# Loading and splitting the first weight and input tiles in a stated order, with a second-half weight buffer of its own

## The chip, the cores and the metric

One core of a Trainium2 chip runs the whole kernel in one launch. The metric is device time in microseconds of an execution; a kernel's time is the median of its runs. The engines are named as in the profile: PE (TensorE, matmuls), PEld (its weight loads), DVE (VectorE), ACT (ScalarE), POOL (GpSimd) and SP (SyncE, which here only issues DMAs). ACT issues DMAs too.

## The reference, cut to what matters

A layer over 1024 tokens of width 1024. The part around the change is the first RMSNorm and the input projection; after it come window attention, neighbourhood attention, an output projection and a gated MLP, which stay as they are.

```python
def rmsnorm(x, g):
    xf = x.astype(jnp.float32)
    y = xf * lax.rsqrt(jnp.mean(xf * xf, axis=-1, keepdims=True) + EPS)
    return (y * g.astype(jnp.float32)).astype(x.dtype)
...
    hn = rmsnorm(h, norm_mix[l])
    proj = jnp.einsum('bsd,de->bse', hn, w_in[l])
```

## The kernel before, in words

**Products in three matmuls.** A float32 operand is split in a high part (a copy on ACT to the type float32r) and a low part (on DVE: the value less its high part). A product of a 128x128 weight block and a 128x512 block of x is then three matmuls (`block`, L143 to L146): high by high, high by low, low by high.

**The head.** x comes transposed, as eight tiles `xt` of 128 x 1024 (k = 0 to 7, each with two halves h of 512 tokens). The first two output tiles of the projection, `first`, are computed side by side, in PSUM banks named `pj` (tile 0) and `o` (tile 1): for each k, for each h, for each of the two tiles, one `block`. That is 96 matmuls. The gain of the norm is multiplied into x as it is split (`split_x` for k = 0 and 1 in halves, `split_scaled` for the rest, giving `xgh` and `xgl`); the inverse root of the mean square is multiplied in when the banks are read out. So the squares of all x tiles are summed beside it (`squares`, L166: a square `sq` on ACT, an add on DVE), reduced on PE (`ss`, L181), rooted on ACT and inverted on DVE (`v`, L184 and L185), spread over the partitions on PE (`sw`, L192) and copied to `rstd1` (L626), which every read-out needs. Between them PE runs the third output tile (banks `s`): its first half before `ss`, 3 of its blocks between `ss` and `sw`, the rest after.

**Weights.** The first halves of the weights of the two tiles (k = 0 to 3) are in `head`, loaded by ACT's queue in four DMAs (L103) and split by `first_w`. The second halves (k = 4 to 7) go through `load_w` (L140): a raw buffer of tag `raw`, which has two slots, then a high and a low buffer of tags `whi` and `wlo`, which have three slots each (L135). A slot is taken again when its last reader is done.

**Order.** PE runs in program order. The other engines' and the queues' order is set by a scheduler, from priorities and its own estimates; each engine then runs its list in order and stops at an instruction whose data or buffer isn't ready. A DMA also waits for the landing of the one eight before it. The warm-up matmuls (L114, WARM of them) run on PE ahead of the data.

**What stands next to it.** `nsink` (L592) is made on DVE from the sinks; POOL copies it into probability tiles (L348). POOL also builds the bias tiles `xb` (L426 and L427, `bias_tiles`) from `rr`, a load of 244.5 KB by SP (L418) into one single buffer. The next weights (projections 3 and 4) are loaded by SP at L130 and split at L136 and L137; on ACT the first split for projection 4 stands just ahead of the root `v`.

Of the kernel before, what the change touches and what calls it, by code (L numbers as in the profile page):

```python
# [13 lines left out]
F32 = mybir.dt.float32  # L14
F32R = mybir.dt.float32r
AF = mybir.ActivationFunctionType
ALU = mybir.AluOpType
PSUM = bass.MemoryType.PSUM

D, S, HD = 1024, 1024, 64  # L20
KT = D // 128
# [6 lines left out]
EPS = 1e-6  # L28
# [6 lines left out]
SPARE = (3, 6)  # L35
AHEAD = 2
EVA = (1, 3, 5, 8)
WARM = 8

REST = 11  # L40

# [6 lines left out]
C_NMIX, C_NFFN, C_NFIN, C_NA, C_NB, C_CW, C_CB, C_SINK = 0, 8, 16, 24, 28, 32, 98, 120  # L48
C_END = 128
# [4 lines left out]
def hybrid_layer(tc, xT, w_in, w_out, w_gate, w_up, w_down, small, sink, rpb, consts, rope, out):  # L54
    nc = tc.nc
    with ExitStack() as ctx:
        pool = lambda name, bufs, **kw: ctx.enter_context(tc.tile_pool(name=name, bufs=bufs, **kw))
        cpool = pool("const", 1)
# [4 lines left out]
        wpool = inner("weights", 3)  # L63
# [6 lines left out]
        def big(name, tag, dt=F32):  # L70
            return lpool.tile([128, S], dt, name=name, tag=tag, bufs=slots[tag])

        def tmp(name, dt=F32, n=S):
            return tpool.tile([128, n], dt, name=name, tag="t", padded_shape=[128, S + 2])

        def bank(name, tag):
            return psum.tile([128, HALF], F32, name=name, tag=tag)

        f32 = lambda ap: ap.bitcast(F32)
        tsl = lambda h: slice(h * HALF, (h + 1) * HALF)  # L80
        col = lambda c: par[:, c:c + 1]

        par = cpool.tile([128, C_END], F32, name="par")
        nc.scalar.dma_start(par[:, 0:C_SINK], small)
        ones = cpool.tile([128, 128], F32, name="ones")
        nc.gpsimd.memset(ones, 1.0 / D)
        eps = cpool.tile([128, 1], F32, name="eps")
        nc.gpsimd.memset(eps, EPS)
        cst = cpool.tile([128, K_END], F32, name="cst")
        ident = cst[:, K_ID:K_ID + 128]  # L90


        def load_x(k, parts=1):
            xt = big("xt", "op")
            n = S // parts
            for i in range(parts):
                nc.sync.dma_start(xt[:, i * n:(i + 1) * n], xT[k, :, i * n:(i + 1) * n])
            return xt

        head = [[wpool.tile([128, 4, 128], dt, name="w0", tag=tag, bufs=n) for dt, tag, n in ((F32, "raw", 2), (F32R, "whi", 3), (F32R, "wlo", 3))] for _ in range(2)]  # L100
        for ks in (slice(0, 1), slice(1, 4)):
            for m, (raw, _, _) in enumerate(head):
                nc.scalar.dma_start(raw[:, ks], w_in[m, :, ks, :])  # L103
        xts = [load_x(0, 2), load_x(1, 2)]


        ctx.enter_context(tc.manual_schedule(engines={mybir.EngineType.PE}))


        warm = cpool.tile([128, 1], F32, name="warm")  # L110
        nc.scalar.activation(warm, eps, AF.Square)
        warm_ps = psum.tile([128, HALF], F32, name="warm_ps", tag="pt")
        for _ in range(WARM):
            nc.tensor.matmul(warm_ps[:, 0:128], ones, ones, start=True, stop=True)  # L114
# [12 lines left out]
        def fetch_w(src):  # L127

            raw = wpool.tile([128, 4, 128], F32, name="raw", tag="raw", bufs=2)
            nc.sync.dma_start(raw, src)  # L130
            return raw

        def halve_w(raw):

            hi, lo = (wpool.tile([128, 4, 128], F32R, name=n, tag=n) for n in ("whi", "wlo"))  # L135
            mark["weights"] = nc.scalar.activation(hi, raw, AF.Copy)  # L136
            mark["weights low"] = nc.vector.tensor_tensor(lo, raw, f32(hi[:, :, :]), op=ALU.subtract)  # L137
            return [(hi[:, j, :], lo[:, j, :]) for j in range(4)]

        def load_w(src):  # L140
            return halve_w(fetch_w(src))

        def block(ps, w, x, h, first, last):  # L143
            nc.tensor.matmul(ps, w[0], x[0][:, tsl(h)], start=first, stop=False)  # L144
            nc.tensor.matmul(ps, w[0], x[1][:, tsl(h)], start=False, stop=False)  # L145
            nc.tensor.matmul(ps, w[1], x[0][:, tsl(h)], start=False, stop=last)  # L146
# [6 lines left out]

        def split_scaled(src, scale, name, tag):
            hi, lo = big(name + "h", tag, F32R), big(name + "l", tag, F32R)
            nc.scalar.activation(hi, src, AF.Copy, scale=scale)
            nc.vector.scalar_tensor_tensor(lo, src, scale, f32(hi[:, :]), op0=ALU.mult, op1=ALU.subtract)
            return hi, lo

        def split(src, name, tag):  # L160
            hi, lo = big(name + "h", tag, F32R), big(name + "l", tag, F32R)
            nc.scalar.activation(hi, src, AF.Copy)
            nc.vector.tensor_tensor(lo, src, f32(hi[:, :]), op=ALU.subtract)
            return hi, lo

        def squares(tiles, engine):  # L166
            acc = None
            for t in tiles:
                s2 = tmp("sq")
                nc.scalar.activation(s2, t, AF.Square)  # L170
                if acc is not None:
                    engine.tensor_tensor(s2, s2, acc, op=ALU.add)
                acc = s2
            return acc
# [114 lines left out]
        mix = [None] * 8  # L289
# [269 lines left out]
        xg, first = [None] * KT, [Project(0), Project(1)]  # L559

        def split_x(k, h):

            g = col(C_NMIX + k)
            hi, lo = (t[:, tsl(h)] for t in xg[k])
            nc.scalar.activation(hi, xts[k][:, tsl(h)], AF.Copy, scale=g)
            nc.vector.scalar_tensor_tensor(lo, xts[k][:, tsl(h)], g, f32(hi), op0=ALU.mult, op1=ALU.subtract)

        def first_w(ks):
            for raw, hi, lo in head:
                nc.scalar.activation(hi[:, ks], raw[:, ks], AF.Copy)  # L570
                nc.vector.tensor_tensor(lo[:, ks], raw[:, ks], f32(hi[:, ks]), op=ALU.subtract)

        for k in range(2):
            xg[k] = big("xgh", "xg", F32R), big("xgl", "xg", F32R)
        split_x(0, 0)
        first_w(slice(0, 1))
        split_x(0, 1)
        first_w(slice(1, 4))
        for h in range(2):
            split_x(1, h)  # L580
        for p, (_, hi, lo) in zip(first, head):
            p.w = [(hi[:, j, :], lo[:, j, :]) for j in range(4)]
        for k in range(2, 4):
            xts.append(load_x(k))
        for p in first:
            p.w += load_w(w_in[p.m, :, 4:8, :])
        for k in range(4, KT):
            xts.append(load_x(k))
        nc.sync.dma_start(cst, consts)
        nc.sync.dma_start(par[:, C_SINK:C_END], sink.partition_broadcast(128))  # L590
        nsink = cpool.tile([128, 8], F32, name="nsink")
        nc.vector.tensor_scalar(nsink, par[:, C_SINK:C_END], -1.0, None, op0=ALU.mult)  # L592
        quarters = lambda t: t[:, :].rearrange("p (a s w) -> p a s w", a=4, s=2)
        turns = quarters(big("turns", "mix"))
        rc, rs = turns[:, 0], turns[:, 1]
        nc.sync.dma_start(turns[:, 0:2], rope)
        t = quarters(big("f", "mix"))
        folded += [(t[:, 0], t[:, 1]), (t[:, 2], t[:, 3]), (turns[:, 2], turns[:, 3])]

        banks = [[bank("pj", "pj") for _ in range(2)], [bank("o", "o") for _ in range(2)]]  # L600
        acc = None
        for k in range(KT):
            if k > 1:
                xg[k] = split_scaled(xts[k], col(C_NMIX + k), "xg", "xg")
            for h in range(2):
                for p, ps in zip(first, banks):
                    block(ps[h], p.w[k], xg[k], h, k == 0, k == KT - 1)
        acc = squares(xts, nc.vector)
        jobs = [Project(m) for m in range(2, 18)] + [OutA(d) for d in range(KT)]
        third = jobs[0]  # L610
        raw, hi, lo = big("raw3", "mix"), big("whi3", "mix", F32R), big("wlo3", "mix", F32R)
# [114 lines left out]
        for g in range(2):  # L726
            for b in range(NB):
                q, t = unit_window(g, b)
# [49 lines left out]
        for u in range(len(flat)):  # L778
            q, t, need, kind = flat[u]
# [49 lines left out]
        for h in range(2):  # L829
            wide = widen(vb2[h], "pt")  # L830
            for i in range(4):
                x = mix[4 + i][:, tsl(h)]
                hi, lo = (t[:, tsl(h)] for t in mg[4 + i])
# [303 lines left out]
        raws, dws, xs, xraw, kept, sum_tiles = {}, {}, {}, {}, {}, {}  # L1137
# [116 lines left out]
        sq, todo, vs = {}, [], {}  # L1254
# [57 lines left out]
        for i, (p, j, c) in enumerate(order):  # L1312
            prepare(i + 6, i + 4)
            f, n = PARTS[c]
# [30 lines left out]
        parts = {}  # L1345
# [15 lines left out]
        first = quarters[1].start  # L1361
# [96 lines left out]
```

## Time and profile before

| | |
|---|---|
| runs | 1103.87, 1103.57, 1101.68 us; median 1103.57 |
| profiled execution | 1103.74 us, of which 1101.9 us from the first to the last instruction (span) |
| granted TensorE clock, mean | 0.996 |
| busy share of the span | PE 98%, PEld 82%, DVE 78%, ACT 50%, POOL 10% |
| DMA | 144.95 MB moved |

A row of the timeline has the start and the duration in us, the engine (a q behind it: its queue of DMA issues), the line in the kernel, the operation, what it writes and reads, its shape and count, and in brackets how long the engine stood idle before it and what ended that. A row of windows has the stretch, its length, the busy time and the number of instructions for PE, PEld, DVE, ACT and POOL, then the granted clock, the DMA engines' busy share and GB/s.

### The profile page before, as it was taken

Reading aid. Unit: us, or ns where it says so; the run is one execution under the profiler, and the core shown is the slowest. Engines: PE = TensorE matmul, PEld = TensorE weight load, DVE = VectorE, ACT = ScalarE, POOL = GpSimd, SP = SyncE. Lnnn points to the kernel's source line nnn. Section 1 sums busy time; section 2 is a strip of 40 time slices with the busy share of each in tenths; the row PEclk is TensorE's granted clock in tenths of the full one; section 3 lists DMA queues with packets and bytes.
Section 4 is the critical chain, followed back from the end, with each engine's and each line's share of the span. In section 5 each row is a group of like instructions: output and inputs, shape, how many; then the busy total and the mean of one; then the engine's idle time right before and its main releaser. Section 6 shows DMA issues by size and latency. Waiting matters only on the chain.

```text
span 1101.9 us, 15051 instructions
## 1 busy us (share of the span) xinstructions
PE 1079.2 (98%) x5190; PEld 901.0 (82%) x5190; DVE 858.5 (78%) x1565; ACT 552.9 (50%) x1042; POOL 109.2 (10%) x188
## 2 busy tenths in 40 slices
PE   8999999999999999999999999999999999999996
PEld 6888788888888888887788888888888778888886
DVE  7688787667688689899988877887787857886843
ACT  7457676556676544545434343433434643533631
POOL 2223333222232100000000000000000000000001
PEclk9999999999999999999999999999999999999998
DMA  7222122222225136214342232322233888774824
GB/s 271 72 72 68 48 58 68 77 76 77 77 67 159 68 127 240 96 39 162 124 161 89 104 124 77 132 98 106 96 112 109 277 288 289 258 227 165 270 79 154
DMA packets 68365, 144.95 MB, mean 132 GB/s; under 512 B 8128, under 2 KB 18880, under 8 KB 68288
## 3 DMA queue, kind: packets, MB, share of 16 engines
q1 hardware_dynamic: 57632, 118.16, 33.6%
q10 hardware_dynamic: 10656, 25.82, 6.2%
q8 instruction: 41, 0.67, 0.2%
q14 instruction: 36, 0.29, 0.1%
HBM read 103.58 MB, written 28.57 MB: 120 GB/s over the span
## 4 chain that ended last, share of the span: by engine, by line
PE 86%; DVE 7%; DMA 3%; ACT 2%; issue 2%; POOL 0%; SPq 0%; DVEq 0%; ACTq 0%; POOLq 0%
PE pj L144 7%; PE pj L145 7%; PE pj L146 7%; PE dn L866 6%; PE dn L867 6%; PE dn L868 6%; PE z L868 5%; PE z L866 5%; PE z L867 5%; PE x L866 3%; PE s L327 3%; PE x L867 3%; PE x L868 3%; PE y L868 3%; PE y L867 3%; PE y L866 3%
## 5 line engine op out<-in xcount | busy, mean ns | idle before, releaser
L866 PE MATMUL dn<-xd,whi 128*128 128x512 f32 (+1 forms) x330 | 124.9, 378 | 2.3 <-ACT c L1294 2.3
L868 PE MATMUL dn<-xd,wlo 128*128 128x512 f32 (+1 forms) x330 | 124.4, 377 | 0.0
L867 PE MATMUL dn<-xd,whi 128*128 128x512 f32 (+1 forms) x330 | 124.2, 377 | 0.0
L855 ACT ACTIVATE whi<-ws 128x512 fp32r<-128x512 f32 (+1 forms) x100 | 60.2, 624 | 122.3 <-DVE ws L972 80.4
L866 PE MATMUL z<-hg,whi 128*128 128x512 f32 x264 | 103.0, 390 | 1.0 <-DVE gs L1022 1.0
L144 PE MATMUL pj<-xgh,whi 128*128 128x512 f32 x248 | 104.0, 419 | 0.0
L868 PE MATMUL z<-hg,wlo 128*128 128x512 f32 x264 | 103.1, 390 | 0.6 <-DVE wlo L856 0.6
L867 PE MATMUL z<-hg,whi 128*128 128x512 f32 x264 | 102.7, 389 | 0.0
L353 ACT ACTIVATE p<-p,nm 128x385 f32<-128x385 f32 (+3 forms) x128 | 75.3, 588 | 51.7 <-DVE nm L349 50.6
L146 PE MATMUL pj<-xgh,wlo 128*128 128x512 f32 x248 | 97.6, 393 | 0.0
L145 PE MATMUL pj<-xgl,whi 128*128 128x512 f32 x248 | 97.2, 392 | 0.0
L357 POOL TENSOR_SCALAR p<-p,sm 128x384 f32<-128x384 f32 (+1 forms) x128 | 74.1, 591 | 215.9 <-DVE sm L355 201.5
L856 DVE TENSOR_TENSOR wlo<-raw,whi 128x512 fp32r<-128x512 f32 (+1 forms) x102 | 66.6, 673 | 22.7 <-ACT whi L855 22.4
L363 DVE TENSOR_TENSOR pl<-pt,ph 128x384 fp32r<-128x384 f32 (+2 forms) x108 | 63.0, 588 | 24.5 <-ACT ph L362 23.2
L855 ACT ACTIVATE whi<-raw 128x512 fp32r<-128x512 f32 (+1 forms) x102 | 60.5, 613 | 42.7 <-DMA raw<-in_w_down_dram 19.3
L856 DVE TENSOR_TENSOR wlo<-ws,whi 128x512 fp32r<-128x512 f32 (+1 forms) x100 | 66.8, 683 | 18.7 <-ACT whi L855 18.7
L1285 POOL TENSOR_TENSOR h<-h,wide 128x256 f32<-128x256 f32 (+1 forms) x6 | 5.4, 920 | 718.7 <-ACT wide L1281 718.7
L1177 ACT ACTIVATE xd<-xd 128x512 fp32r<-128x512 f32 x77 | 47.1, 627 | 55.0 <-DMA xd<-x 53.5
L866 PEld LDWEIGHTS dn<-xd,whi 128*128 128x128 f32 x330 | 62.5, 189 | 14.0 <-ACT c L1294 2.8
L868 PEld LDWEIGHTS dn<-xd,wlo 128*128 128x128 f32 x330 | 62.4, 189 | 11.5
L867 PEld LDWEIGHTS dn<-xd,whi 128*128 128x128 f32 x330 | 62.5, 190 | 11.1
L362 ACT ACTIVATE ph<-pt 128x384 fp32r<-128x384 f32 (+2 forms) x108 | 55.2, 515 | 32.0 <-PE pt L462 25.0
(211 smaller groups left out, 2686.0 us busy)
## 6 DMA issues: line engine op xcount, KB each, us to landing
xd<-x SPq DMA_DIRECT2D x77, 256.0 KB, 5.1
raw<-in_w_down_dram SPq DMA_DIRECT2D x72, 256.0 KB, 3.4
raw<-in_w_gate_dram SPq DMA_DIRECT2D x22, 512.0 KB, 3.6
raw<-in_w_up_dram SPq DMA_DIRECT2D x22, 512.0 KB, 3.8
x<-c ACTq DMA_DIRECT2D x22, 512.0 KB, 2.6
raw<-in_w_in_dram SPq DMA_DIRECT2D x32, 256.0 KB, 3.0
raw<-in_w_down_dram SPq DMA_DIRECT2D x36, 192.0 KB, 3.9
x<-t ACTq DMA_DIRECT2D x11, 512.0 KB, 2.6
```

The costliest lines, as they stand in the source:

```text
L144: nc.tensor.matmul(ps, w[0], x[0][:, tsl(h)], start=first, stop=False)
L145: nc.tensor.matmul(ps, w[0], x[1][:, tsl(h)], start=False, stop=False)
L146: nc.tensor.matmul(ps, w[1], x[0][:, tsl(h)], start=False, stop=last)
L353: nc.scalar.activation(p[:, j, 0:e], p[:, j, 0:e], AF.Exp, bias=nm, scale=-1.0, accum_out=sm[:, j:j + 1])
L357: nc.gpsimd.tensor_scalar(p[:, i, 0:m], p[:, i, 0:m], sm[:, i:i + 1], 1.0, op0=ALU.mult, op1=ALU.mult)
L362: nc.scalar.activation(ph[:, 0:n], ps[:, 0:n], AF.Copy)
L363: nc.vector.tensor_tensor(pl[:, 0:n], ps[:, 0:n], f32(ph[:, 0:n]), op=ALU.subtract)
L855: nc.scalar.activation(hi, src, AF.Copy)
L856: nc.vector.tensor_tensor(lo, src, f32(hi[:, :, :]), op=ALU.subtract)
L866: nc.tensor.matmul(ps, w[0], x[0], start=first and i == 0, stop=False, skip_group_check=True)
L867: nc.tensor.matmul(ps, w[0], x[1], start=False, stop=False, skip_group_check=True)
L868: nc.tensor.matmul(ps, w[1], x[0], start=False, stop=last and i == len(ws) - 1, skip_group_check=True)
```

## The change

All x tiles and weights of the head are queued in one stated order, and `tc.keep_in_program_order` (`pin`) keeps the marked instructions of a queue or an engine in the order in which the program states them.

- The four first-half weight DMAs move from ACT's queue to SP's, behind the first half of x tile 0; the second half of x tile 0 moves to ACT's queue.
- The second halves of both tiles' weights are loaded into a buffer of their own, `second` (one of the eight slots of tag `mix`), each behind its x tile (2 and 3). They are still split by `halve_w`, into `whi` and `wlo`.
- x is split for k = 2 to 7 ahead of the matmul loop; with each of k = 4 to 7 go two squares and their adds (`add_square`), in place of `squares` after the loop.
- `nsink` and the loads of the constants are pinned too, in the place where the program has them.
- WARM goes from 8 to 9.

```diff
-WARM = 8
+WARM = 9
...
+        pin = tc.keep_in_program_order
         par = cpool.tile([128, C_END], F32, name="par")
+        xts = [big("xt", "op") for _ in range(KT)]
+
+        def load_x(k, part=slice(0, S), queue=nc.sync):
+            pin(queue.dma_start(xts[k][:, part], xT[k, :, part]))
+
+        second = big("raws", "mix")[:, :].rearrange("p (m k c) -> p m k c", m=2, c=128)
+        load_x(0, tsl(0))
         nc.scalar.dma_start(par[:, 0:C_SINK], small)
+        load_x(0, tsl(1), nc.scalar)
+        for ks in (slice(0, 1), slice(1, 4)):
+            for m, (raw, _, _) in enumerate(head):
+                pin(nc.sync.dma_start(raw[:, ks], w_in[m, :, ks, :]))
+        load_x(1, tsl(0))
+        load_x(1, tsl(1))
+        for k in (2, 3):
+            load_x(k)
+            pin(nc.sync.dma_start(second[:, k - 2], w_in[k - 2, :, 4:8, :]))
+        for k in range(4, KT):
+            load_x(k)
...
+        def add_square(t, acc):
+            s2 = tmp("sq")
+            pin(nc.scalar.activation(s2, t, AF.Square))
+            if acc is not None:
+                pin(nc.vector.tensor_tensor(s2, s2, acc, op=ALU.add))
+            return s2
...
         for k in range(2, 4):
-            xts.append(load_x(k))
-        for p in first:
-            p.w += load_w(w_in[p.m, :, 4:8, :])
+            xg[k] = split_scaled(xts[k], col(C_NMIX + k), "xg", "xg")
+            first[k - 2].w += halve_w(second[:, k - 2])
+        added = None
         for k in range(4, KT):
-            xts.append(load_x(k))
-        nc.sync.dma_start(cst, consts)
-        nc.sync.dma_start(par[:, C_SINK:C_END], sink.partition_broadcast(128))
+            xg[k] = split_scaled(xts[k], col(C_NMIX + k), "xg", "xg")
+            for i in range(2 * k - 8, 2 * k - 6):
+                added = add_square(xts[i], added)
+        pin(nc.sync.dma_start(cst, consts))
+        pin(nc.sync.dma_start(par[:, C_SINK:C_END], sink.partition_broadcast(128)))
         nsink = cpool.tile([128, 8], F32, name="nsink")
-        nc.vector.tensor_scalar(nsink, par[:, C_SINK:C_END], -1.0, None, op0=ALU.mult)
+        pin(nc.vector.tensor_scalar(nsink, par[:, C_SINK:C_END], -1.0, None, op0=ALU.mult))
...
         for k in range(KT):
-            if k > 1:
-                xg[k] = split_scaled(xts[k], col(C_NMIX + k), "xg", "xg")
             for h in range(2):
                 for p, ps in zip(first, banks):
                     block(ps[h], p.w[k], xg[k], h, k == 0, k == KT - 1)
-        acc = squares(xts, nc.vector)
+        acc = added
```

In the changed kernel the line numbers are 7 higher from the helpers on, and 14 higher behind `add_square`; the split of weights is at L143 and L144, that of x at L163 and L164, the squares at L175 and their adds at L177, the bias loads at L432.

More of the change, by code (lines that the diff above doesn't have):

```diff
@@ L81, in hybrid_layer @@
         col = lambda c: par[:, c:c + 1]
+        pin = tc.keep_in_program_order
         par = cpool.tile([128, C_END], F32, name="par")
-        nc.scalar.dma_start(par[:, 0:C_SINK], small)
+        xts = [big("xt", "op") for _ in range(KT)]
+        def load_x(k, part=slice(0, S), queue=nc.sync):
+            pin(queue.dma_start(xts[k][:, part], xT[k, :, part]))
+        head = [[wpool.tile([128, 4, 128], dt, name="w0", tag=tag, bufs=n) for dt, tag, n in ((F32, "raw", 2), (F32R, "whi", 3), (F32R, "wlo", 3))] for _ in range(2)]
+        second = big("raws", "mix")[:, :].rearrange("p (m k c) -> p m k c", m=2, c=128)
+        load_x(0, tsl(0))
+        nc.scalar.dma_start(par[:, 0:C_SINK], small)
+        load_x(0, tsl(1), nc.scalar)
[9 more added lines that the diff above has]
+            load_x(k)
+        cst = cpool.tile([128, K_END], F32, name="cst")
+        ident = cst[:, K_ID:K_ID + 128]
+        ctx.enter_context(tc.manual_schedule(engines={mybir.EngineType.PE}))
         ones = cpool.tile([128, 128], F32, name="ones")
@@ L88, in hybrid_layer @@
         nc.gpsimd.memset(eps, EPS)
[L89 to L107, printed above, removed]
         warm = cpool.tile([128, 1], F32, name="warm")
-        nc.scalar.activation(warm, eps, AF.Square)
+        pin(nc.scalar.activation(warm, eps, AF.Square))
         warm_ps = psum.tile([128, HALF], F32, name="warm_ps", tag="pt")
@@ L155, in split_scaled @@
             hi, lo = big(name + "h", tag, F32R), big(name + "l", tag, F32R)
-            nc.scalar.activation(hi, src, AF.Copy, scale=scale)
-            nc.vector.scalar_tensor_tensor(lo, src, scale, f32(hi[:, :]), op0=ALU.mult, op1=ALU.subtract)
+            pin(nc.scalar.activation(hi, src, AF.Copy, scale=scale))
+            pin(nc.vector.scalar_tensor_tensor(lo, src, scale, f32(hi[:, :]), op0=ALU.mult, op1=ALU.subtract))
             return hi, lo
@@ L564, in split_x @@
             hi, lo = (t[:, tsl(h)] for t in xg[k])
-            nc.scalar.activation(hi, xts[k][:, tsl(h)], AF.Copy, scale=g)
-            nc.vector.scalar_tensor_tensor(lo, xts[k][:, tsl(h)], g, f32(hi), op0=ALU.mult, op1=ALU.subtract)
+            pin(nc.scalar.activation(hi, xts[k][:, tsl(h)], AF.Copy, scale=g))
+            pin(nc.vector.scalar_tensor_tensor(lo, xts[k][:, tsl(h)], g, f32(hi), op0=ALU.mult, op1=ALU.subtract))
         def first_w(ks):
             for raw, hi, lo in head:
-                nc.scalar.activation(hi[:, ks], raw[:, ks], AF.Copy)
-                nc.vector.tensor_tensor(lo[:, ks], raw[:, ks], f32(hi[:, ks]), op=ALU.subtract)
+                pin(nc.scalar.activation(hi[:, ks], raw[:, ks], AF.Copy))
+                pin(nc.vector.tensor_tensor(lo[:, ks], raw[:, ks], f32(hi[:, ks]), op=ALU.subtract))
         for k in range(2):
@@ L595, in hybrid_layer @@
         rc, rs = turns[:, 0], turns[:, 1]
-        nc.sync.dma_start(turns[:, 0:2], rope)
+        pin(nc.sync.dma_start(turns[:, 0:2], rope))
         t = quarters(big("f", "mix"))
@@ L600, in hybrid_layer @@
         banks = [[bank("pj", "pj") for _ in range(2)], [bank("o", "o") for _ in range(2)]]
-        acc = None
         for k in range(KT):
-            if k > 1:
-                xg[k] = split_scaled(xts[k], col(C_NMIX + k), "xg", "xg")
             for h in range(2):
```

## The prediction

> **What bounds the kernel now.** I read the page first, then busy time by stretch for the first 61 us, which is all the change touches, then the timeline there, engine by engine.
>
> ```profile
> PE 1079.2 (98%) x5190; PEld 901.0 (82%) x5190; DVE 858.5 (78%) x1565; ACT 552.9 (50%) x1042; POOL 109.2 (10%) x188
> ...
> 5.47:8.42 2.95, 2.67 (x9) 1.53 (x9) 2.17 (x6) 2.11 (x5) 0.00 (x0) 1.00 1.02 336
> 8.42:18.60 10.18, 10.18 (x44) 7.73 (x42) 8.53 (x11) 9.36 (x11) 0.00 (x0) 1.00 1.02 402
> 18.60:21.00 2.40, 1.46 (x5) 0.78 (x5) 2.40 (x4) 2.40 (x4) 0.00 (x0) 1.00 0.73 284
> 21.00:30.31 9.31, 9.31 (x42) 7.69 (x41) 9.21 (x10) 6.59 (x8) 8.59 (x5) 1.00 0.29 90
> 30.31:39.60 9.29, 9.29 (x51) 7.99 (x50) 2.29 (x5) 2.45 (x4) 4.62 (x7) 1.00 0.27 83
> ```
>
> TensorE is the bound: 98% of the span, and all of the stretches after 21 us. Only the head has holes, and there ACT and DVE are full (2.40 of 2.40). Undisturbed, matmuls of 512 columns follow each other at 0.227 us (seven steps from 16.79 to 18.37 below). The 96 of the first two tiles need 21.8 us; they take from 5.47 to 30.31, 24.8. So 3.1 us is the most that removing head stalls can bring, plus what an earlier start gives.
>
> ```profile
> 0.73 0.41 ACTq L84 DMA_DIRECT2D par<-in_small_dram  x1
> ...
> 3.11 1.28 ACT L111 ACT_TABLE_LOAD   x1 [3.11 <-issue]
> 4.51 0.71 ACT L565 ACTIVATE xgh<-xt,par 128x512 fp32r<-128x512 f32 x1
> 5.47 0.50 PE L144 MATMUL pj<-xgh,w 128*128 128x512 f32 x1 [1.02 <-ACT w L570]
> 6.31 0.31 ACT L570 ACTIVATE w<-w 128x128 fp32r<-128x128 f32 x1 [0.90 <-DMA w<-in_w_in_dram]
> 7.28 0.75 DVE L566 SCALAR_TENSOR_TENSOR xgl<-xt,par,xgh 128x512 fp32r<-128x512 f32 x1 [0.32 <-ACT xgh L565]
> 10.04 1.15 ACT L156 ACTIVATE xgh<-xt,par 128x1024 fp32r<-128x1024 f32 x1 [0.74 <-DMA xt<-in_xT_dram]
> 12.57 0.50 PE L145 MATMUL pj<-xgl,w 128*128 128x512 f32 x1
> ```
>
> **Part 1, the start: about 0.3 us gained (0 to 0.8).** ACT issues five DMAs before its table load at 3.11; now two. Three issues less, 0.48 each (3.11 less 0.73 in five), lets the load end near 2.9 instead of 4.39, so the first split at 4.51 waits only for its data, about 4.0, and the first matmul comes near 5.05. The four weight DMAs move to SP ahead of the second x tile; the weights that ACT awaited until 6.31 land about 0.9 earlier, so the split chain on DVE (7.28) moves by 0.8. But the third x tile landed at 10.0 with the queues full, and the same bytes stand ahead of it now: I let it land 0.3 earlier, so the matmul at 12.57 and what follows moves by 0.3. The ninth warm-up pair fits in the idle before 5.47.
>
> **Part 2, the second halves of the weights.** They land in a buffer of their own, so SP no longer waits for the head's raw buffers, and the next two weight loads go out early. Their split is another matter. Tags whi and wlo still have three slots: four tiles want them. The fourth, tile 1's second half, takes tile 0's first, whose last reader is the k=3 product with xgl. In the changed program's order ACT has this split (L143) directly behind xgh of k=3 and ahead of xgh of k=4; before, it stood behind xgh of k=6.
>
> ```profile
> 13.81 1.14 ACT L156 ACTIVATE xgh<-xt,par 128x1024 fp32r<-128x1024 f32 x1
> 14.85 1.05 ACT L170 ACTIVATE sq<-xt 128x1024 f32<-128x1024 f32 x1
> 15.80 1.14 ACT L156 ACTIVATE xgh<-xt,par 128x1024 fp32r<-128x1024 f32 x1
> 16.79 0.39 PE L145 MATMUL pj<-xgl,w 128*128 128x512 f32 x1
> 18.37 0.39 PE L146 MATMUL pj<-xgh,wlo 128*128 128x512 f32 x1
> 18.84 0.62 ACT L136 ACTIVATE whi<-raw 128x512 fp32r<-128x512 f32 x1
> 19.36 1.05 ACT L170 ACTIVATE sq<-xt 128x1024 f32<-128x1024 f32 x1
> 19.51 0.50 PE L144 MATMUL o<-xgh,whi 128*128 128x512 f32 x1 [0.75 <-ACT whi L136]
> 20.43 0.50 PE L146 MATMUL o<-xgh,wlo 128*128 128x512 f32 x1 [0.19 <-DVE wlo L137]
> ```
>
> Before, the split came late (18.84) and PE waited from 18.60 to 19.51 and again for wlo until 20.43. The change removes that, 1.5 us. It puts a longer wait in its place: ACT is done with k=3 near 13, then stands until the matmul at 16.79 ends (17.2, less 0.3). Queued behind it are xgh of k=4 and everything else on ACT; before, xgh of k=4 was done at 14.95. Split at about 16.95, xgh of k=4 0.52 later (18.84 to 19.36): call its start A = 17.5.
>
> From A the order is fixed: per k one xgh, two squares on ACT; one xgl, two adds on DVE, the adds chained.
>
> ```profile
> 25.02 1.23 DVE L614 TENSOR_TENSOR wlo<-raw,whi 128x1024 fp32r<-128x1024 f32 x1
> 26.16 1.23 DVE L172 TENSOR_TENSOR sq<-sq 128x1024 f32<-128x1024 f32 x1
> 27.89 2.59 DVE L172 TENSOR_TENSOR sq<-sq 128x1024 f32<-128x1024 f32 x2
> ```
>
> ACT steps are 1.04 (13.81 to 14.85) and 0.95 (14.85 to 15.80); DVE steps 1.14 (25.02 to 26.16), and 1.34 between chained adds (2.59 for two). ACT: squares A+1.04, A+1.99, xgh5 A+2.94. DVE: xgl4 A+1.19, add A+3.1 (it waits for the second square), xgl5 4.24, adds 5.37 and 6.71, xgl6 7.84, adds 8.97 and 10.31, xgl7 11.44 to 12.72. DVE needs 3.6 us for a k, PE 2.72 (12 x 0.227), so PE waits for xgl each time: k=5 at A+5.56, k=6 at 9.17, k=7 at 12.78. Then 0.34 and ten steps: the third projection starts at A+15.4 = 32.9, against 30.31: **+2.6 us** (2.1 to 2.9 with part 1's bounds). The squares are pinned between the splits; before, several ran after the last one.
>
> **Part 3, POOL and SP behind nsink.** nsink now stands last among the adds on DVE, so the scheduler has put both bias builds (L426, L427, two ops each) ahead of the nsink copies on POOL, and SP's order is: two weight loads, bias load rr three times, then the weight load for projection 4, which before stood ahead of the second rr. rr has one buffer: the third load waits for the second build, the second for the first.
>
> ```profile
> L348 POOL COPY p<-nsink x5: 181/1110/6400, 21.7 to 29.3; 128x2 f32<-128x2 f32 x5
> ...
> 22.77 7.76 POOL L348 COPY p<-nsink 128x2 f32<-128x2 f32 x4
> 33.09 0.57 SPq L418 DMA_DIRECT2D rr<-in_rpb_dram  x1
> 33.76 1.00 SPq L130 DMA_DIRECT2D raw<-in_w_in_dram  x2
> 37.04 0.97 POOL L426 TENSOR_TENSOR xb<-cst,rr 128x384 f32<-128x384 f32 x1 [3.98 <-DMA rr<-in_rpb_dram]
> 37.97 0.72 POOL L427 TENSOR_TENSOR xb<-cst,rr 128x256 f32<-128x256 f32 x1
> ```
>
> A copy of 256 numbers, 0.18 us at its shortest, took 6.40 from 22.77: it stood while DVE ran one op with two SBUF operands upon another, and ended at 29.17, as the first of the two chained adds (27.89 + 1.23) was over and the second not begun.
>
> When does the first rr land? Ahead of it go 7.2 MB; from 2 us on, at 336 GB/s until 8.4 and 402 after (the windows above), they take until 21; I say 22 for the last of the 16 engines, and 2.3 for rr itself: 24.3 (23.5 to 25), an estimate. The first build (0.97 and 0.72) then gets in where the DVE chain pauses between an add and what depends on it, near 25.4 and 28.7, and holds DVE up by 1.6: third projection 34.5. rr again at 29.5, landed 3.95 later (33.09 to 37.04). DVE then runs without a gap until nsink, 35.1; the second build ends near 37.8. Third rr at 37.85, the weight load behind it on the same queue: landed after 3.95 and about 0.6 for its own bytes, 42.4. Who needs it?
>
> ```profile
> 28.02 0.35 SPq L130 DMA_DIRECT2D raw<-in_w_in_dram  x1
> 30.66 0.63 ACT L136 ACTIVATE whi<-raw 128x512 fp32r<-128x512 f32 x1 [0.37 <-DMA raw<-in_w_in_dram]
> 31.31 1.28 ACT L184 ACT_TABLE_LOAD   x1
> 36.74 0.27 ACT L184 ACTIVATE v<-ss,eps 128x4 f32<-128x4 f32 x1 [4.15 <-PE ss L181]
> 37.03 0.18 DVE L185 RECIPROCAL v<-v 128x4 f32<-128x4 f32 x1 [4.55 <-ACT v L184]
> 39.59 1.95 PE L192 MATMUL sw<-cst,v 128*128 128x128 f32 x16
> ```
>
> Its split stands on ACT ahead of the table load and of the root v, on DVE ahead of the reciprocal, and PE's widening sw waits for that. Before, v had 4.15 us to spare. Now: 42.4, split and load 0.65 + 1.28, root and reciprocal 0.5: sw at 44.9. PE alone would be there at 34.5 + 9.28 = 43.8. Against 39.59: **+5.3 us**, not added to the 2.6 but in its place, as the later of two ends. After sw all engines keep the old order and PE its steps, so I carry the shift to the end. The profiled execution took 1103.74 (its span 1101.9); its sum is 1109.0. The median, 1103.57, stands 0.2 below, within the range of the three runs, so I give **1109.0**.
>
> **Rivals.** (a) The bias loads are hidden: POOL gets its turn at every end of a DVE op. The second build then ends near 36, the weights land at 40.6 and sw is ready at 43.1, before PE's 43.8. Parts 1 and 2 and the builds' time on DVE remain, +2.6 to +4.2: 1106.3 to 1107.9. The 6.40 us, over five DVE ends, speaks against it. The Trainium skill (SBUF — State Buffer, "SBUF: two separate sides") tells of an exclusive lock on the ports that DVE and GpSimd share, and measured "blocked until DVE-end + ~115 ns". By that rule this rival holds; the trace agrees on the blocking, not on its length. 17%.
>
> (b) POOL stays shut out: a port that comes free only at chained adds gives the first build one op at 27.7 and the other at nsink, near 35.3; second build 41.7, load 46.3, sw 48.8, +9.2, and PE stands 5 us.
>
> ```profile
> 904.55 0.50 PE L866 MATMUL dn<-xd,whi 128*128 128x512 f32 x1 [2.33 <-ACT c L1294]
> 905.00:909.00 4.00, 4.00 (x13) 3.10 (x12) 4.00 (x8) 3.70 (x7) 0.00 (x0) 0.57 0.83 261
> ```
>
> After the 2.33 us stall at 904.55 the granted clock was 0.57 over four us, so about 1.7 us (0.43 of four) more can follow: up to 1114.6. 15%.
>
> (c) Faster: ACT's wait does not bite. That needs xgh of k=4 to be late anyway, x landing after PE's k=3; then the stalls go and 3.1 + 0.4 less: 1100.2. Against it: before, xgh of k=4 started at 13.81, data landed. 4%.
>
> (d) Gains and losses cancel, the head's 0.8 kept whole and DVE never last: within 0.2% (2.2 us, about what a measurement here tells from no change). 8%.
>
> **Numbers.** My case has 56%, 1107.9 to 1110.2. The range takes in (a) and the lower part of (b): 1106.0 to 1112.5. Faster 0.04, same 0.08, slower 0.88.
>
> **What would show it.** ACT idle some 3 to 4 us before whi at L143, ended by PE pj; PE waiting for xgh of k=4 near 18.6, then for xgl each k; third projection at 33 to 35; POOL's second build after 35; whi of projection 4 waiting for its DMA past 41; sw near 45. Wrong if ACT passes the fourth whi before PE's k=3, or if sw comes before 42.

## The result, and the profile after

The changed kernel takes 1107.87 us in the median of six runs, the kernel before 1101.92 beside it: ratio 1.0049, 95% interval 1.0031 to 1.0066. A second comparison gave 1108.25 (seven runs) against 1102.60 (32 runs): 1.0048, 1.0029 to 1.0066. By the medians it is slower by 5.65 to 5.95 us; the forecast was 1109.0, that is +5.3. (The ratio is the comparison's own estimate; the quotients of the medians, 1.0054 and 1.0051, lie within its intervals.)

The timeline of the changed kernel, ACT from 11 us on (in its code the split of a whole x tile is L163, of second-half weights L143, a square L175):

```profile
11.78 1.15 ACT L163 ACTIVATE xgh<-xt,par 128x1024 fp32r<-128x1024 f32 x1 [0.23 <-DMA xt<-in_xT_dram]
17.05 0.63 ACT L143 ACTIVATE whi<-raws 128x512 fp32r<-128x512 f32 x1 [4.12 <-PE pj L152]
17.59 1.13 ACT L163 ACTIVATE xgh<-xt,par 128x1024 fp32r<-128x1024 f32 x1
18.63 1.99 ACT L175 ACTIVATE sq<-xt 128x1024 f32<-128x1024 f32 x2
```

After k=3 ACT stands 4.12 us at the fourth whi, until PE's product with xgl (L152) gives back the slot; xgh of k=4 starts at 17.59 (before: k=4 at 13.81). PE then waits for that xgh, for its xgl and, later, for the xgl of k=7 (first three rows; the last is the third projection's first matmul, 30.31 before):

```profile
18.78 0.49 PE L151 MATMUL pj<-xgh,whi 128*128 128x512 f32 x1 [0.85 <-ACT xgh L163]
20.10 0.50 PE L152 MATMUL pj<-xgl,whi 128*128 128x512 f32 x1 [0.83 <-DVE xgl L164]
...
31.73 0.50 PE L152 MATMUL pj<-xgl,whi 128*128 128x512 f32 x1 [1.14 <-DVE xgl L164]
...
34.39 0.39 PE L151 MATMUL s<-xgh,whi 128*128 128x512 f32 x1
```

POOL's bias builds (L440, L441) and the DVE operations that fell beside them:

```profile
24.40 2.00 POOL L440 TENSOR_TENSOR xb<-cst,rr 128x384 f32<-128x384 f32 x1 [23.43 <-DMA rr<-in_rpb_dram]
26.36 1.71 POOL L441 TENSOR_TENSOR xb<-cst,rr 128x256 f32<-128x256 f32 x1
31.68 1.98 POOL L440 TENSOR_TENSOR xb<-cst,rr 128x384 f32<-128x384 f32 x1 [3.62 <-DMA rr<-in_rpb_dram]
33.62 1.71 POOL L441 TENSOR_TENSOR xb<-cst,rr 128x256 f32<-128x256 f32 x1
...
25.45 2.02 DVE L164 SCALAR_TENSOR_TENSOR xgl<-xt,par,xgh 128x1024 fp32r<-128x1024 f32 x1
27.40 3.08 DVE L177 TENSOR_TENSOR sq<-sq 128x1024 f32<-128x1024 f32 x2
30.39 1.28 DVE L164 SCALAR_TENSOR_TENSOR xgl<-xt,par,xgh 128x1024 fp32r<-128x1024 f32 x1
```

Each build takes twice as long as alone (2.00 against 0.97, 1.71 against 0.72 in the kernel before), and the DVE operation beside it loses time too: an xgl takes 2.02 instead of 1.28. The second build is over at 35.33. The end of the head:

```profile
16.47 19.42 SPq L432 DMA_DIRECT2D rr<-in_rpb_dram  x3
37.11 4.53 SPq L137 DMA_DIRECT2D raw<-in_w_in_dram  x3
...
39.93 0.63 ACT L143 ACTIVATE whi<-raw 128x512 fp32r<-128x512 f32 x1 [5.63 <-DMA raw<-in_w_in_dram]
40.58 1.28 ACT L198 ACT_TABLE_LOAD   x1
41.87 0.42 ACT L198 ACTIVATE v<-ss,eps 128x4 f32<-128x4 f32 x2
...
43.77 1.95 PE L206 MATMUL sw<-cst,v 128*128 128x128 f32 x16
```

SP holds the weights of projection 4 behind the third rr, until 37.11; ACT stands 5.63 us for them. The roots are done at 42.3, yet sw shows no wait in front of it: it comes 9.38 behind the third projection, the time of PE's own work (9.28 before). So in this execution PE's lateness, +4.18 at sw (43.77 against 39.59), is the whole loss of the head.

The landmarks of every kernel told of below, from their profiles (us; "k=2": the first product with xgl of the third x tile; "third": the third projection's first matmul):

| kernel | k=2 | third | sw | median, runs | ratio to before, 95% |
|---|---|---|---|---|---|
| before | 12.57 | 30.31 | 39.59 | 1101.92 to 1102.60 | |
| before, second profile | 13.77 | 30.26 | 39.53 | | |
| changed | 12.41 | 34.39 | 43.77 | 1107.87, 6 | 1.0049 (1.0031 to 1.0066) |
| changed, second profile | 13.63 | 35.43 | 45.37 | 1108.25, 7 | 1.0048 (1.0029 to 1.0066) |
| own buffer | 13.49 | 31.54 | 41.73 | 1104.64, 10 | 1.0023 (1.0005 to 1.0040) |
| split stated later | 13.44 | 32.27 | 42.53 | 1106.19, 10 | 1.0030 (1.0011 to 1.0049) |
| squares last | 13.13 | 35.37 | 44.65 | 1106.00, 10 | 1.0040 (1.0022 to 1.0058) |
| bias loads held | 13.48 | 34.15 | 43.42 | 1107.40, 10 | 1.0040 (1.0024 to 1.0056) |
| own buffer, held | 13.05 | 29.89 | 39.16 | 1102.45, 12 | 1.0000 (0.9983 to 1.0017) |
| and squares spread | 13.89 | 30.12 | 39.39 | 1102.24, 12 | 0.9993 (0.9977 to 1.0008) |
| and x tile 2 in halves | 12.24, 11.71 | 28.39, 27.92 | 37.66, 37.19 | 1100.87, 1101.80, 12 each | 0.9991 (0.9973 to 1.0008), 0.9994 (0.9976 to 1.0012) |
| start alone on before | 12.89 | 29.84 | 39.12 | 1102.31, 10 | 1.0007 (0.9991 to 1.0022) |
| own buffer on before | 12.62 | 28.85 | 38.12 | 1100.75, 12 | 0.9993 (0.9979 to 1.0007) |

### The profile page after: what moved, and what is told of

Its sections match the earlier page's. It is cut to its first block, busy times and chain, and to the rows that moved or that the text cites. A ratio compares the mean times of both kernels' runs of the same rounds, so it can differ in the third digit from the quotient of the medians.

```text
span 1104.3 us, 15055 instructions
## 1 busy us (share of the span) xinstructions
PE 1080.6 (98%) x5192; PEld 902.1 (82%) x5192; DVE 860.6 (78%) x1565; ACT 552.7 (50%) x1042; POOL 105.2 (10%) x188
## 4 chain that ended last, share of the span: by engine, by line
PE 87%; DVE 7%; ACT 2%; issue 2%; DMA 2%; POOL 0%; SPq 0%; DVEq 0%; ACTq 0%; POOLq 0%
PE pj L152 7%; PE pj L151 7%; PE pj L153 7%; PE dn L879 6%; PE dn L880 6%; PE dn L881 6%; PE z L881 5%; PE z L879 5%; PE z L880 5%; PE s L341 3%; PE x L879 3%; PE x L881 3%; PE x L880 3%; PE y L881 3%; PE y L880 3%; PE y L879 3%
## 5 line engine op out<-in xcount | busy, mean ns | idle before, releaser
L152 PE MATMUL pj<-xgl,whi 128*128 128x512 f32 x248 | 97.8, 395 | 2.0 <-DVE xgl L164 2.0
```

## The experiments

The theory: ACT's wait for the slot makes the loss, with DVE's 3.6 us for a k behind it and the builds on DVE's time on top. Rivals: the pinned order of squares and adds alone; the builds alone.

**Own buffer.** The wait goes, all else stays.

```diff
-            first[k - 2].w += halve_w(second[:, k - 2])
+            if k == 2:
+                first[0].w += halve_w(second[:, 0])
+            else:
+                own = big("wown", "mix", F32R)[:, :].rearrange("p (s j c) -> p s j c", s=2, c=128)
+                pin(nc.scalar.activation(own[:, 0], second[:, 1], AF.Copy))
+                pin(nc.vector.tensor_tensor(own[:, 1], second[:, 1], f32(own[:, 0]), op=ALU.subtract))
+                first[1].w += [(own[:, 0, j, :], own[:, 1, j, :]) for j in range(4)]
```

> The changed kernel with one edit: tile 1's second weight half is split into a buffer of its own, so ACT does not stand for a slot that PE still reads; squares, bias loads and queues stay. Theory 'slot wait': xgh of k=4 starts near 13.95 instead of 17.6 (its x tile has landed by then), the DVE chain behind it moves by as much, PE no longer waits for k=4, and the third projection starts near 30.4 instead of 34.4 (29.3 if the builds on GpSimd no longer fall on DVE's last pieces). Then the weights of projection 4, queued behind the third bias load, land near 38.5 and PE's widening sw, free at 39.6, stands about 1 us: near 40.8, +1.2 us over the kernel before, about 1103. Theory 'DVE's order' (the pinned squares and adds set the end whatever ACT does): third projection still past 33, about 1106 to 1107. Theory 'GpSimd's builds': nothing moves but by 1 us, about 1107.

Measured: +2.1 us (medians) where the changed kernel has +5.65 to +5.95. ACT, PE and, at the end, ACT and PE again:

```profile
13.97 0.61 ACT L603 ACTIVATE wown<-raws 128x512 fp32r<-128x512 f32 x1
14.89 1.15 ACT L163 ACTIVATE xgh<-xt,par 128x1024 fp32r<-128x1024 f32 x1 [0.31 <-DMA xt<-in_xT_dram]
...
28.88 0.50 PE L152 MATMUL pj<-xgl,whi 128*128 128x512 f32 x1 [1.49 <-DVE xgl L164]
...
31.54 0.39 PE L151 MATMUL s<-xgh,whi 128*128 128x512 f32 x1
...
39.26 0.63 ACT L143 ACTIVATE whi<-raw 128x512 fp32r<-128x512 f32 x1 [9.97 <-DMA raw<-in_w_in_dram]
...
41.73 1.49 PE L206 MATMUL sw<-cst,v 128*128 128x128 f32 x11 [0.75 <-DVE v L199]
```

ACT passes the split without a wait, and PE's two stalls at k=4 are gone. What is left is DVE's lateness at the last xgl (1.65 us), where the builds fell, and then the weights of projection 4: sw now waits for the reciprocal, 0.91 us over PE's 9.28. The third projection came at 31.54, not 30.4: the third x tile had landed 1.1 late (below), and with that taken off it is the expected value. DVE's order as the only cause is out.

**Split stated later.** Three slots as in the change, the fourth split two x tiles later in the stated order.

```diff
-            first[k - 2].w += halve_w(second[:, k - 2])
+            if k == 2:
+                first[0].w += halve_w(second[:, 0])
...
+            if k == 5:
+                first[1].w += halve_w(second[:, 1])
```

> The changed kernel with the same three slots, but tile 1's second half is split two x tiles later in the stated order, behind the split of k=5. Theory 'slot wait': ACT reaches the split near 17.9, when PE has left the slot, so it waits for nothing; xgh of k=4 starts near 13.95; PE waits a little for whi and wlo (about 1.3 us in sum, as before the change); third projection near 31, sw near 41 (about +1.4), about 1103.5. Theory 'DVE's order': third projection past 33, about 1106 to 1107. If the slot itself, and not the place in the order, made the wait, it stays with 3 to 4 us and the time is that of the changed kernel, about 1107.5.

```profile
15.06 1.15 ACT L163 ACTIVATE xgh<-xt,par 128x1024 fp32r<-128x1024 f32 x1 [1.06 <-DMA xt<-in_xT_dram]
16.12 1.99 ACT L175 ACTIVATE sq<-xt 128x1024 f32<-128x1024 f32 x2
18.02 1.14 ACT L163 ACTIVATE xgh<-xt,par 128x1024 fp32r<-128x1024 f32 x1
19.06 0.62 ACT L143 ACTIVATE whi<-raws 128x512 fp32r<-128x512 f32 x1
```

ACT waits for x and not for the slot of the fourth split. Third projection 32.27, three fifths of the way from the changed kernel's 35.43 (with much the same landing) to 30.31. So three slots alone don't make the wait; the place in the order does. The time followed less than expected: 1106.19, not 1103.5, and an interval that overlaps the changed kernel's. PE still waits for the fourth wlo (0.77 at 21.23) and for the last xgl (0.88 at 29.65), and sw for the reciprocal (0.82).

**Squares last.** The squares unpinned and behind the matmul loop again, the wait kept.

```diff
-            for i in range(2 * k - 8, 2 * k - 6):
-                added = add_square(xts[i], added)
...
-        acc = added
+        acc = squares(xts, nc.vector)
```

> The changed kernel with the slot wait kept, but the squares and their sums are no longer stated between the splits; the scheduler puts most of them behind the last split. Theory 'slot wait and then DVE at 3.6 us for a k': xgh of k=4 still starts near 17.5, but DVE now needs only 1.2 us for a k and PE catches up at its own pace after one stall of 1.2 to 2 us: third projection near 31.0 to 31.8 (34.4 in the changed kernel), sw near 40.3 to 41. About +1.5 us over the kernel before, 1103.5. Theory 'the ACT wait alone' (the pitch of DVE plays no part): third projection near 34, no change against the changed kernel, 1107.5. Theory 'the pinned squares alone': third near 30.3 and the kernel before's time.

A miss as a test. The scheduler moved squares ahead of the fourth whi, so DVE had three adds to do before the xgl of k=4, and PE's granted clock halved after two stalls:

```profile
15.92 3.88 DVE L186 TENSOR_TENSOR sq<-sq 128x1024 f32<-128x1024 f32 x3
...
19.85 0.50 PE L151 MATMUL pj<-xgh,whi 128*128 128x512 f32 x1 [1.00 <-ACT xgh L163]
21.65 0.79 PE L152 MATMUL pj<-xgl,whi 128*128 128x512 f32 x1 [1.30 <-DVE xgl L164]
```

The windows from there on:

```profile
21.65:27.90 6.25, 6.25 (x15) 4.90 (x16) 6.25 (x5) 4.62 (x6) 3.42 (x2) 0.50 0.10 24
```

From 21.65 on PE waits for no xgl any more, which speaks for the pitch; but the third projection at 35.37 holds some 3 us of half clock (half of 6.25), and the 32.3 that is left mixes a late landing with the moved adds. The three theories aren't told apart by it.

**Bias loads held.** The wait and the pinned squares stay; the loads of rr go behind the rotations' transfers, so that no build runs in the head.

```diff
-            nc.sync.dma_start(raw, src)
+            with behind("back"):
+                nc.sync.dma_start(raw, src)
```

> The changed kernel with the bias loads held on their queue until the loads' group behind the first rotations, so that the builds on GpSimd leave the first 36 us; slot wait and squares stay. Theory 'the builds take DVE's time, about 0.7 to 1 us for each of two that fall on the chain': third projection near 33.0 (34.4 in the changed kernel), sw near 42.3: 1.4 us faster than the changed kernel, about 1106. Theory 'the builds run beside DVE': third projection stays at 34.4, no change. Theory 'bias loads hold up the weights of projection 4 on SP' (as the prediction had it): those land earlier than 39.9, but PE at sw does not move by it, as it stood for nothing there.

```profile
18.11 0.63 ACT L143 ACTIVATE whi<-raws 128x512 fp32r<-128x512 f32 x1 [4.08 <-PE pj L152]
18.65 1.13 ACT L163 ACTIVATE xgh<-xt,par 128x1024 fp32r<-128x1024 f32 x1
...
27.85 0.50 PE L152 MATMUL pj<-xgl,whi 128*128 128x512 f32 x1 [0.64 <-DVE xgl L164]
...
31.52 0.50 PE L152 MATMUL pj<-xgl,whi 128*128 128x512 f32 x1 [0.65 <-DVE xgl L164]
...
34.15 0.39 PE L151 MATMUL s<-xgh,whi 128*128 128x512 f32 x1
```

Here part 2 stands by itself. From A = 18.65 the prediction's steps give k=6 at A+9.17 = 27.82, k=7 at A+12.78 = 31.43, the third projection at A+15.4 = 34.05: each within 0.1 of the row. PE waits at both for an xgl, 3.67 apart: DVE's pitch. With the builds, the third projection came at A+16.80 and A+16.58 in the two profiles of the changed kernel: they cost 1.1 to 1.3 us. Over the kernel before, the medians have 4.9 us for 5.65 to 5.95: the same direction, less than the intervals can tell, and less than the 1.4 us expected.

**The changed kernel again.**

> The changed kernel itself, a second time, beside the others of this call. What is open: its profiled execution accounts for +4.2 us up to sw, its runs for +5.4 to 5.9. In three of the four profiles of the first experiments the third x tile landed 1.0 to 1.1 us later than in that execution (10.9 against 9.86), by one of the 16 DMA engines. Theory 'landing': here the third x tile lands near 10.9 too, the first xgl product of k=2 comes near 13.4 instead of 12.41, and everything behind it, up to the third projection, 1.0 later: near 35.4, and about 1107.5 to 1108. Theory 'clock': k=2 comes at 12.4 as before, and the difference is in how long the halved clock lasts. In any case about +5 us over the kernel before.

```profile
11.11 1.15 ACT L163 ACTIVATE xgh<-xt,par 128x1024 fp32r<-128x1024 f32 x1 [0.52 <-DMA xt<-in_xT_dram]
...
18.31 0.63 ACT L143 ACTIVATE whi<-raws 128x512 fp32r<-128x512 f32 x1 [4.12 <-PE pj L152]
...
34.61 1.75 DVE L627 TENSOR_TENSOR wlo<-raw,whi 128x1024 fp32r<-128x1024 f32 x1
...
36.41 0.50 PE L153 MATMUL s<-xgh,wlo 128*128 128x512 f32 x1 [0.36 <-DVE wlo L627]
```

"Landing" holds. The third x tile was there at 11.11 instead of 9.88 (first profile), k=2 came at 13.63, and with it ACT's slot (18.31) and the third projection, 35.43. DVE, later by as much, then brought the wlo of the third projection late too (0.53 us). sw at 45.37: +5.78 against the first profile of before, +5.84 against the second. Of the two profiles the second, +5.8, has what the medians lost (5.65 to 5.95); the first, +4.2, has 1.5 us less.

**The kernel before again.**

> The kernel before itself, profiled a second time, to see how far its own head moves from one execution to the next. In its first profile the third x tile landed at 10.02, the first xgl product of k=2 came at 12.57, the third projection at 30.31 and sw at 39.59. If a late DMA engine is a matter of the execution, k=2 comes anywhere from 12.5 to 13.6 here and the third projection less than that later, since PE stands for tile 1's second half at 18.6 anyway (30.3 to 31.0); if the late landing belongs to the changed queue order, k=2 is at 12.6 within 0.2 again.

Windows of the same stretch, first profile:

```profile
5.73:10.50 4.77, 4.49 (x17) 2.78 (x17) 3.78 (x8) 3.44 (x7) 0.00 (x0) 1.00 1.01 363
```

and second:

```profile
5.73:10.50 4.77, 4.77 (x11) 3.86 (x12) 3.77 (x8) 3.47 (x7) 0.00 (x0) 1.00 1.02 360
```

Neither theory had the cause. x landed as before (ACT waited for it until 10.00); PE, though busy throughout, did 11 matmuls in place of 17, 0.43 us each, the step that it has at half clock (as from 20.75 to 23.31 in the changed kernel's first profile, with 0.52 granted; here the trace has no granted clock before 10.5 us, so the column's 1.00 says nothing). So k=2 came 1.2 us later, and the third projection at the same 30.26: PE had less to stand for tile 1's second half, which ACT split at 18.80 as ever. **The stall that the change removes was a cover: it took up what came late ahead of it.** In the changed kernel ACT's split follows PE's k=3, so the same lateness goes straight through (k=2 1.22 later, third 1.04 later).

**Own buffer and held loads together**, then with one square for each of the last four k, then with the third x tile loaded and split in halves. The edits behind the first two:

```diff
-            for i in range(2 * k - 8, 2 * k - 6):
+            for i in {4: (0,), 5: (1,), 6: (2,), 7: (3,)}[k]:
                 added = add_square(xts[i], added)
+        for i in range(4, KT):
+            added = add_square(xts[i], added)
```

```diff
-            load_x(k)
+            for h in range(2 if k == 2 else 0):
+                load_x(2, tsl(h))
+            if k == 3:
+                load_x(3)
...
-        for h in range(2):
-            split_x(1, h)
+        for k in (1, 2):
+            for h in range(2):
+                split_x(k, h)
```

> The changed kernel with a buffer of its own for tile 1's second half (as in the first experiment) and the bias loads held behind the rotations. Theory 'slot wait, builds on DVE's time, bias load ahead of projection 4's weights, each with its own share': third projection at 29.9 with a late third x tile (31.54 with the buffer alone, less the 1.65 us that PE stood for the last xgl there), 28.8 with an early one; sw 9.28 behind it, at 38.1 to 39.2, not held by the weights of projection 4; 0.4 to 1.5 us faster than the kernel before, about 1101 to 1102. Rival 'the pinned squares alone cost, builds or not': PE still waits 1 us or more for the last xgl, third near 30.5 to 31, sw near 40, about 1103.

> As the run before it, with one square for each of the last four k instead of two, the other four behind the last split: DVE then needs 2.4 us for a k, less than PE's 2.72. Theory: where the buffer and the held bias loads leave DVE's 3.6 us for a k as the end that comes last, this gives 0.3 to 0.7 us more at the third projection (28.7 to 29.7, set by the landing of the third x tile alone); where PE no longer waited, nothing. About 1.0 to 1.7 us faster than the kernel before: 1100.8 to 1101.5. Rival: the squares moved behind the splits come late for the mean squares ss, and PE waits there: no gain or a loss.

> As the run before it, with the third x tile loaded and split in halves like the first two. Theory 'the landing of the third x tile sets the start': the first product with its xgl needs only the half, 0.43 us of ACT and 0.5 us of DVE less, so it comes 0.8 us earlier (11.7 for 12.4 with an early landing, 12.6 for 13.4 with a late one), and the third projection as much: near 28.0 to 28.9; some 2 us faster than the kernel before, about 1100. Rival 'the last DMA engine brings both halves late': 0.2 us or nothing.

> The version of the last experiment (buffer of its own, bias loads held, one square for a k, third x tile in halves) a second time, beside the others: its head should again bring sw near 37.7 to 38.7 against 39.59, and 1 to 2 us less than the kernel before; the first comparison left open whether it is faster.

PE's last wait of the 96 and the third projection, in the timeline of the first of these kernels:

```profile
27.27 0.50 PE L152 MATMUL pj<-xgl,whi 128*128 128x512 f32 x1 [0.32 <-DVE xgl L164]
...
29.89 0.39 PE L151 MATMUL s<-xgh,whi 128*128 128x512 f32 x1
```

of the second (squares spread):

```profile
13.89 0.50 PE L152 MATMUL pj<-xgl,w 128*128 128x512 f32 x1 [0.56 <-DVE xgl L164]
...
30.12 0.39 PE L151 MATMUL s<-xgh,whi 128*128 128x512 f32 x1
```

and of the third (halves):

```profile
10.75 0.50 PE L155 MATMUL pj<-xgl,w 128*128 128x512 f32 x1 [0.28 <-DVE xgl L584]
...
28.39 0.39 PE L154 MATMUL s<-xgh,whi 128*128 128x512 f32 x1
```

With both suspects gone the head ends where it did before the change (sw 39.16, ratio 1.0000): the loss is accounted for. Spreading the squares takes away the last wait for DVE, but here x came late (k=2 at 13.89), so the end hardly moved. With halves PE waits for nothing behind 10.75: sw 1.9 and, in the second profile, 2.4 us ahead of the kernel before. In the whole time this isn't shown, twice: both intervals hold 1. In the second profile PE stood longer behind the head (1.07 us for a transfer kb at 351.08, 1.02 at 450.74 and 3.76 at 906.46, where the first profile has one such wait, 1.25 at 902.24), and single runs of one kernel spread over more than 8 us (1097.88 to 1106.52).

**One part alone, on the kernel before.** The start (queues and WARM), and the buffer without anything else:

```diff
-        for p in first:
-            p.w += load_w(w_in[p.m, :, 4:8, :])
+        first[0].w += load_w(w_in[0, :, 4:8, :])
+        own, fresh = big("wown", "mix", F32R)[:, :].rearrange("p (s j c) -> p s j c", s=2, c=128), fetch_w(w_in[1, :, 4:8, :])
+        nc.scalar.activation(own[:, 0], fresh, AF.Copy)
+        nc.vector.tensor_tensor(own[:, 1], fresh, f32(own[:, 0]), op=ALU.subtract)
+        first[1].w += [(own[:, 0, j, :], own[:, 1, j, :]) for j in range(4)]
```

> The kernel before with part 1 of the change alone: the weight loads of the first two tiles on SP ahead of the second x tile, the second half of the first x tile on ACT's queue, nine warm-up pairs. The splits' order stays the scheduler's, which now puts tile 1's second half behind xgh of k=5, and two squares ahead of the splits of the second and third x tile. Theory 'landing sets k=2, start gains 0 to 0.3': first matmul near 4.9 (5.47 before), k=2's first xgl product 12.4 to 13.6, PE then stands for tile 1's second half for 1 to 1.5 us, third projection 29.5 to 31; within 0.2% of the kernel before. Rival 'the 0.6 us of the first matmul are kept': third 29.5 or earlier whatever lands when.

> The kernel before with one edit: tile 1's second weight half is split into a buffer of its own; start, queues, squares and bias loads stay as they were (the scheduler puts this split directly behind that of tile 0). Theory 'slot': the stalls of PE between 18.60 and 21.0 go, and k=2's first xgl product at 12.6 (to 13.4 with a late landing) sets the third projection 16.4 later: 29.0 to 29.8 against 30.31; sw 38.3 to 39.1, 0.5 to 1.3 us faster than the kernel before. Rival 'DVE is then last anyway' (wlo of the third projection, squares): PE stands there instead, no change.

Timeline of the buffer alone, ACT and PE:

```profile
13.29 0.63 ACT L136 ACTIVATE whi<-raw 128x512 fp32r<-128x512 f32 x1
13.96 0.63 ACT L587 ACTIVATE wown<-raw 128x512 fp32r<-128x512 f32 x1
...
28.85 0.39 PE L144 MATMUL s<-xgh,whi 128*128 128x512 f32 x1
```

and its window from PE's last wait on:

```profile
8.07:28.85 20.78, 20.78 (x90) 16.66 (x90) 19.07 (x21) 18.45 (x21) 7.05 (x6) 1.00 0.74 277
```

The start alone: first matmul 5.10, but k=2 at 12.89, and the kernel before's time. The buffer alone, five lines: no stall of PE from 8.07 on (20.78 of 20.78), sw 1.47 us earlier, median 1.28 us less; the interval, 0.9979 to 1.0007, still holds 1.

## Why the prediction was right or wrong

Sign and size were right, the size in part by luck: one step was wrong, and an error the other way hid that.

**Part 1, the start.** Mis-sized. The first matmul did come early (4.86; 5.05 forecast, 5.47 before), but at k=2 "0.3 us gained, 0 to 0.8" was 0.16 in the first profile and a loss of 1.06 in the second, both against 12.57; the six other kernels with the new queue order and a whole third tile have losses too (k=2 at 13.05 to 13.89). Against the second profile of the kernel before (13.77, half clock), all but the 13.89 are early. Among the seven profiles with the whole new queue order in which ACT's row shows the wait for the third x tile, it ended at 9.88 once and at 10.53 to 11.36 six times; with the old order at 10.04, 10.00 and 10.09. The bytes ahead of the tile are the same; why it landed later was not tested.

**Part 2, the wait.** Right: A = 17.59 against 17.5, and with the builds away each of its later steps to 0.1 us. From A to the third projection the held kernel took 15.50 us (15.4 forecast); put on A = 17.59 that is 33.1, or +2.8 for the forecast's +2.6, within its 2.1 to 2.9. The slot as the cause is shown by the own buffer, its place in the order by the later split. (The prediction's "3.1 us" for the stalls of the head is 3.0 by its own figures, 24.8 less 21.8; only rival (c) used it.)

**Part 3, the builds on DVE.** Right on the landing of the first rr (24.40 for 24.3) and on the cost, which was forecast slightly high: 1.1 to 1.3 us for 1.6.

**Part 3, SP behind the builds.** This step failed. I let DVE run "without a gap until nsink, 35.1", the second build end near 37.8, the weights land at 42.4, sw wait until 44.9. The rows have 35.33, 39.93 and an sw at PE's own 43.77: POOL came in at the end of a DVE operation each time, as rival (a) had it, whose range reached +4.2. The first build's second operation, forecast to get in near 28.7, was over at 28.07. In the second profile the weights were split at 40.95, and sw showed no wait either. The copy of 6.40 us, on which I turned (a) down, was no guide to the builds. The chain itself is real: with PE earlier (own buffer) it did hold sw up, by 0.91.

**The total.** 1.1 too much from SP and up to 1.4 too little from the landing, which the change no longer covers, left a forecast within 1.2 us of the medians. That the two nearly cancel is luck. By its steps the first profile belongs to rival (a) and not to my case. The profiled executions differ by 2.3 us only (1106.08 and 1103.74) since the kernel before lost some 1.7 us in its own to half clock near 905, which the changed one did not.

## What to carry to other kernels

Stating an order by hand gives up the scheduler's place for each instruction: before placing a split that takes a used slot among pinned instructions, find the slot's last reader, and everything queued behind the split on its engine. (The split that waited here has no pin of its own: `halve_w` states it between the pinned splits of x, and the scheduler put it there on ACT.) A stall on the bound engine may also be the cover for what comes late ahead of it; a change that removes it, or ties another engine to it, makes that lateness count, so compare more than one profile before and after. Where a buffer is what is missing, giving it the buffer and leaving the order alone took PE's stalls away here; a gain in the whole time was not shown.

## What the runs showed of the hardware

- A POOL operation with two SBUF operands that is issued during a DVE operation got in at the end of it, and the DVE operation behind it then ran 0.5 to 0.75 us longer (an xgl 2.02 for 1.28; two adds 3.08 for 2.59). The Trainium skill (SBUF — State Buffer, "A bandwidth-pool intuition that's wrong (but worth ruling out)") has a lock model with "blocked until DVE-end + ~115 ns"; the builds agree. Of the copies p<-nsink most do too: with the own buffer on the kernel before, the five beside DVE's chain took at most 1.20 us each, the time to the next end of a DVE operation. But with the start alone one took 2.31, and in both profiles of the kernel before one stood 6.40 us, over five ends. What sets these apart stays open.
- The same pair of stalls at k=4 (1.02 and 1.09 us over the step of 0.227) was followed by half clock in one of three executions (the two of the changed kernel and the one with held bias loads). Windows of the changed kernel, first profile (the second row stands behind a stall of 2.72 us at 908.83):

```profile
20.43:24.00 3.57, 3.57 (x10) 2.79 (x9) 3.35 (x3) 3.57 (x5) 0.00 (x0) 0.52 0.58 164
...
909.00:913.00 4.00, 4.00 (x18) 3.29 (x19) 4.00 (x8) 3.57 (x8) 0.00 (x0) 1.00 0.79 236
```

  Its second profile:

```profile
20.43:24.00 3.57, 2.75 (x13) 2.17 (x12) 2.96 (x3) 3.57 (x5) 0.00 (x0) 1.00 0.69 218
```

  The kernel before had 0.57 behind a stall of 2.33 us at 904.55; the changed one stood 2.72 there and kept 1.00. The Trainium skill (TensorE: Matmul & The Clock Gate, "What's actually happening") tells of a free-running window of about 3.4 us that judges PE; that one stall is punished and the next isn't agrees with it. At 20.43 it cost little: DVE was last at k=6 and k=7 anyway.
